# Encoder layer in split f32 on one core: queues of the out-projection and the head, the prompt's last rows, and the end

## The chip, the cores and the metric

The kernel runs on one core of a Trainium2 chip. TensorE (PE) multiplies, with its weight load (PEld) beside it; VectorE (DVE) and ScalarE (ACT) work on tiles in SBUF and PSUM; GpSimd (POOL) and SyncE (SP) here issue transfers only, which 16 DMA engines carry out; ACT issues some too. The metric is device time in microseconds of an execution.

## The reference

One layer of a hybrid encoder, for two sequences that share all weights: a prompt of 512 rows and a sample of 1024 rows, with 2048 columns, in f32.

```python
h = rms_norm(x, norm_g)
z = h @ w_in                         # 2048 x 5632
c_val, c_glu, c_gate, q, k, v, a_gate = split(z)
conv = silu(layer_norm(depthwise_31(c_val * sigmoid(c_glu)))) @ w_pw * silu(c_gate)
attn = banded_sink_attention(rope(q), rope(k), v, sink) * silu(a_gate)
x = x + concat(conv, attn) @ w_out   # 2048 x 2048
y = rms_norm(x, final_norm_g)        # y_prompt, y_sample
```

## The kernel before, in words

**Split products.** A matmul in full f32 is made of three in a rounded f32 type (fp32r): each operand is split in a high part (made by ACT, line 510) and a low part, the operand less its high part (DVE, line 511), and PE adds high x high, high x low and low x high. The method `parts` issues both. Split weights are tiles `hl`, loaded weights `raw`, split tokens (columns of the normalised input) `t`. Where the input is scaled by the norm's gain on the way, ACT does it at line 514 and DVE at line 515.

**Seven products for eight.** For the sample, a `Unit` takes two blocks of weight columns and two of rows and forms the 2x2 block product in seven products P1 to P7 on sums and differences of blocks instead of eight. `make0` to `make3` make the weight operands (differences by `sub`, line 143); `product` (matmuls at line 207) issues one product, 12 matmuls of 128x512; `tap` takes its result out of PSUM. `load0` and `load1` (lines 123 and 127) fetch the raw blocks. The prompt's products are issued by `Job` (line 669), the first unit by `Plain` (line 349).

**Weights that come twice.** The last stage of the prompt needs the same sums and differences of out-projection weights (`w_out`) as the sample made. So where `self.sums` is set, `make1` stores P5, P6 and P4 and `less2` stores P7 to HBM (`wsum_P`, 256 KB each), 64 stores in 16 units. `e.store` (line 504) issues on SP's queue. `load_columns` and the fetch at line 1668 read back later.

**Partial sums.** An out-projection unit is an `Onto`. It works in two passes over the depth: the first half's units write partial outputs (`part_out`), the second half's load them and add onto them (lines 285 and 304), tile names `u` and `g`. `Onto.begin` issues the load; `Onto.ahead` says how many products ahead of the one that needs it (2 for most; for the first two units of the second half it is set by `for u in over[1][:2]`). In the other projections, partial sums go out on POOL (line 268) and are added in memory by an accumulating transfer (line 501).

**The order of the work.** The order of calls gives a sequence of instructions; a scheduler places each on its engine by priority and by when its inputs are expected, and `issue_after` puts an instruction behind another. Loads and stores on SP are one queue, in which an entry that waits holds back those behind it. Hardware DMA completions rotate over eight semaphores, so an issue may also wait for the eighth before it. Functions hung into `before` and `after[step]` of a unit run when the unit has got to that step.

**Prompt's rows.** After the sample's in-projection the prompt's first blocks follow. The prompt's input rows come in 16 pieces, loaded from `xr_d` by `load_two`; `follow(step)` scales and splits pieces 4 step to 4 step + 3 by `prompt.split`, and the last sample unit's (`end`) steps 0 to 3 call it.

**Head.** `first` issues the loads of the first unit on SP: the gain `norm_g` (loaded where the constants are made, line 566), first weight blocks (`plain.load_some`, line 325), and the sample's input (`part`, line 1888); `e.warm` issues filler matmuls (`pt<-ones_r`, line 559) ahead of and between the first real ones.

**End.** `LastPost.last_run` computes the prompt's out-projection, its last group of products at line 1794 for two row blocks t after another, and ends with the final norm of four blocks of 128 rows. `complete` squares a column group with a running sum (line 1735); with the fourth group it takes the square root (ACT, 1745), its reciprocal (1747) and one Newton step (1746, 1748 to 1750), scales the rows by it (1754, 1756, 1758) and stores 512 KB pieces to `y_p` (1759).

## Time and profile before

| | us |
|---|---|
| three runs, median | 2084.76 |
| three runs, lowest to highest | 2084.57 to 2086.94 |
| profiled execution | 2080.18 |
| its span, first to last instruction | 2078.40 |
| PE busy | 2060.7 (99%) |
| DVE, ACT, POOL busy | 1754.4, 1043.6, 122.6 |
| DMA | 494.55 MB, 237 GB/s over the span |

The span is the part of the profiled execution that the trace covers; 1.78 us lie around it. Busy shares are taken over the whole span; a row of the timeline gives start and duration of an instruction or of a run of like instructions, with the idle time ahead of it and what released it. Tile names are printed without numbers.

### The profile page before, as it was taken

The numbers are of one execution on the slowest core, as the hardware profiler recorded it, in microseconds if no ns is written. First come the engines' busy times: TensorE is split into PE (matmuls) and PEld (weight loads), VectorE is DVE, ScalarE is ACT, GpSimd is POOL, SyncE is SP. The second block draws the span as 40 slices with busy tenths as digits, with TensorE's granted clock in tenths as the row PEclk, the third lists the DMA queues.
The fourth block names the chain that finished last, engine by engine and source line by source line (L and its number), as shares of the span: only waits on it lengthen the run. The fifth ranks groups of instructions, "written<-read, shape, count | busy, mean of one in ns | idle before, by whom it ended". The sixth has DMA issues, their size and how long they took to land.

```text
span 2078.4 us, 27092 instructions
## 1 busy us (share of the span) xinstructions
PE 2060.7 (99%) x9259; PEld 1699.2 (82%) x9259; DVE 1754.4 (84%) x2873; ACT 1043.6 (50%) x1711; POOL 122.6 (6%) x176
## 2 busy tenths in 40 slices
PE   9999999999999999999999999999999999999998
PEld 8888888888888888788888888888888887888886
DVE  8767899998899999999666877767799977998887
ACT  7485445333464434554455777336454343454454
POOL 0111111111111111100000000000000000000000
PEclk9999999999999999999999999999999999999999
DMA  8888886864577767954455555996789899678897
GB/s 288 312 298 256 199 223 221 285 220 160 188 242 192 175 169 183 280 166 156 153 172 187 177 182 183 315 330 234 247 289 300 278 299 293 220 247 298 289 333 277
DMA packets 245819, 494.55 MB, mean 238 GB/s; under 512 B 23600, under 2 KB 84400, under 8 KB 245680
## 3 DMA queue, kind: packets, MB, share of 16 engines
q1 hardware_dynamic: 225136, 445.62, 63.9%
q0 software_dynamic: 19392, 45.10, 9.4%
q10 hardware_dynamic: 1152, 2.10, 0.3%
q8 instruction: 72, 1.18, 0.2%
q14 instruction: 67, 0.55, 0.1%
HBM read 331.77 MB, written 160.96 MB: 237 GB/s over the span
## 4 chain that ended last, share of the span: by engine, by line
PE 48%; DVE 7%; issue 6%; DMA 4%; ACT 2%; POOL 1%; SPq 0%; ACTq 0%; POOLq 0%; DVEq 0%
PE a L669 13%; PE a L207 7%; PE c L669 6%; PE b L669 6%; PE c L207 3%; PE pv L1196 2%; PE a L1835 2%; PE s L1167 2%; PE s L1835 2%; PE b L207 1%; PE pt L1201 1%; DVE hl L511 1%; DVE f L1003 1%; DVE t L511 1%; DVE f L1040 1%
## 5 line engine op out<-in xcount | busy, mean ns | idle before, releaser
L207 PE MATMUL a<-t,hl 128*128 128x512 f32 x2640 | 633.6, 391 | 4.7 <-DVE u L304 3.2
L207 PEld LDWEIGHTS a<-t,hl 128*128 128x128 f32 x2640 | 494.7, 188 | 110.6 <-DVE u L304 3.6
L510 ACT ACTIVATE hl<-raw 128x1024 fp32r<-128x1024 f32 (+3 forms) x334 | 296.1, 890 | 384.5 <-PE c L207 81.6
L511 DVE TENSOR_TENSOR hl<-raw,hl 128x1024 fp32r<-128x1024 f32 (+3 forms) x334 | 338.8, 1015 | 145.8 <-ACT hl L510 144.4
L669 PE MATMUL a<-t,hl 128*128 128x512 f32 x1344 | 328.0, 394 | 0.0
L207 PE MATMUL c<-t,hl 128*128 128x512 f32 x1320 | 319.2, 389 | 0.0
L207 PEld LDWEIGHTS c<-t,hl 128*128 128x128 f32 x1320 | 247.3, 188 | 51.6 <-DVE u L304 0.4
L669 PEld LDWEIGHTS a<-t,hl 128*128 128x128 f32 x1344 | 248.6, 188 | 49.8
L1040 DVE SCALAR_TENSOR_TENSOR f<-f,c_w_dw,f 128x512 f32<-128x512 f32 x248 | 173.9, 750 | 0.3
L669 PE MATMUL b<-t,hl 128*128 128x512 f32 x672 | 164.6, 395 | 2.2 <-DVE hl L511 2.2
L1003 DVE SCALAR_TENSOR_TENSOR f<-f,c_w_dw,f 128x512 f32<-128x512 f32 x232 | 163.7, 748 | 1.2 <-ACT f L998 1.2
L669 PE MATMUL c<-t,hl 128*128 128x512 f32 x672 | 164.2, 393 | 0.3 <-DVE hl L511 0.3
L207 PE MATMUL b<-t,hl 128*128 128x512 f32 x660 | 160.0, 389 | 0.0
L669 PEld LDWEIGHTS b<-t,hl 128*128 128x128 f32 x672 | 126.1, 190 | 28.0 <-DVE hl L511 2.6
L669 PEld LDWEIGHTS c<-t,hl 128*128 128x128 f32 x672 | 124.7, 188 | 25.5 <-DVE hl L511 0.7
L207 PEld LDWEIGHTS b<-t,hl 128*128 128x128 f32 x660 | 123.7, 188 | 25.6
L1032 DVE SCALAR_TENSOR_TENSOR f<-f,w_both,f 128x512 f32<-128x512 f32 x120 | 90.0, 750 | 2.1
L236 ACT ACTIVATE u<-a 128x512 f32<-128x512 f32 x82 | 48.7, 594 | 66.8 <-PE a L207 64.2
L236 ACT ACTIVATE g<-a 128x512 f32<-128x512 f32 x78 | 46.3, 594 | 69.1 <-PE a L207 64.6
L1181 ACT ACTIVATE p<-p,tiny 128x384 f32<-128x384 f32 (+1 forms) x96 | 54.5, 570 | 39.8 <-DVE tiny L1178 27.3
L510 ACT ACTIVATE a<-pt 128x512 fp32r<-128x512 f32 x64 | 37.9, 593 | 66.3 <-PE pt L1201 66.2
L511 DVE TENSOR_TENSOR a<-pt,a 128x512 fp32r<-128x512 f32 x64 | 44.1, 689 | 27.3 <-ACT a L510 26.6
(350 smaller groups left out, 2687.9 us busy)
## 6 DMA issues: line engine op xcount, KB each, us to landing
raw<-w_in SPq DMA_DIRECT2D x170, 512.0 KB, 5.3
raw<-w_out SPq DMA_DIRECT2D x31, 512.0 KB, 5.0
raw<-w_pw SPq DMA_DIRECT2D x24, 512.0 KB, 4.2
wsum_P<-raw SPq DMA_DIRECT2D x47, 256.0 KB, 3.3
raw<-wsum_P SPq DMA_DIRECT2D x18, 512.0 KB, 5.0
f<-x_s SPq DMA_DIRECT2D x16, 512.0 KB, 8.2
g<-wsum_P SPq DMA_DIRECT2D x28, 256.0 KB, 4.2
a<-sum_S SPq DMA_DIRECT2D x24, 256.0 KB, 6.2
```

What stands on the lines that cost most here:

```text
L207: nc.tensor.matmul(acc, hl[:, l, o, j, :], toks[j][:, r], start=name in FRESH and j == 0 and q == 0, stop=name in LAST and j == HALF - 1 a ...
L236: nc.scalar.activation(t, bank, AF.Copy)
L510: nc.scalar.activation(hi, x, AF.Copy)
L511: nc.vector.tensor_tensor(lo, x, hi.bitcast(F32), ALU.subtract)
L669: nc.tensor.matmul(job.acc[0], hl[:, l, kk // HALF, kk % HALF, :], r, start=i == 0 and p == 0, stop=i == nk - 1 and p == 2,)
L1003: nc.vector.scalar_tensor_tensor(t, h[:, j : j + T], w(j), t, ALU.mult, ALU.add)
L1032: nc.vector.scalar_tensor_tensor(m0, odd[:, j : j + H], both(j), m0, ALU.mult, ALU.add)
L1040: nc.vector.scalar_tensor_tensor(out, d[:, j : j + H], w(2 * j + k), out if j else m0, ALU.mult, ALU.add)
L1167: nc.tensor.matmul(ps[:, 0:n], qs[:, x, h], k[y][:, keys], start=p == 0, stop=p == 2)
L1181: nc.scalar.activation(p[:, 0:n], p[:, 0:n], AF.Exp, bias=nm[:, h : h + 1], accum_out=l[:, h : h + 1])
L1196: nc.tensor.matmul(pv, v[x][:, vs], pt[:, y], start=i == 0 and p == 0, stop=i == last and p == 2)
L1835: nc.tensor.matmul(acc[t], self.toks[name, m][:, x, i, t * P : (t + 1) * P], parts[i][l].rearrange("p a b -> p (a b)"), start=fresh and fi ...
```

## The change

**Head.** The sample's first half of its first input piece and `norm_g` are loaded from ACT's queue, which removes them from SP's; 13 filler matmuls are asked for instead of 20. **Weight-sum stores.** The 64 stores in `make1` and `less2` are issued by POOL instead of SP. **Out-projection.** The first two units of the second half have `ahead` 1 instead of 0. **Prompt's rows.** The last four pieces (`follow(3)`) are split at step 6 of the last sample unit instead of step 3, behind the last high and low parts made by then. **End.** `complete` no longer scales; it returns a function that does (`scale`). The first block of a pair is scaled at once, the second behind the next block's add and square. The Newton step takes four instead of five DVE operations after the root, since -0.5 is folded into its inputs. The half that holds the last columns goes first, and a block is stored in three pieces, 512 KB and 256 KB on SP and 256 KB on ACT.

```diff
@@ -154,7 +154,7 @@
         self.sub(r1[:, 1], r1[:, 1], t2)
         if self.sums:
             for name, x in (("P5", r1[:, 0]), ("P6", t2), ("P4", r1[:, 1])):
-                self.e.store(self.sums[name], x)
+                self.e.nc.gpsimd.dma_start(self.sums[name], x)
         t = self.e.hl_tile()
         for o, x in enumerate((r1[:, 0], t2)):
             self.e.parts(t[:, 0, o], t[:, 1, o], x)
@@ -163,7 +163,7 @@
     def less2(self):
         self.sub(self.r2[:, 0], self.r2[:, 1], self.r2[:, 0])
         if self.sums:
-            self.e.store(self.sums["P7"], self.r2[:, 0])
+            self.e.nc.gpsimd.dma_start(self.sums["P7"], self.r2[:, 0])
         self.lessened = True

     def make2(self):
@@ -508,6 +508,7 @@
         nc = self.nc
         if g is None:
             nc.scalar.activation(hi, x, AF.Copy)
+            self.high_made = nc.cur_bb.bb.instructions[-1]
             nc.vector.tensor_tensor(lo, x, hi.bitcast(F32), ALU.subtract)
             self.low_made = nc.cur_bb.bb.instructions[-1]
         else:
@@ -566,7 +567,7 @@
             nc.sync.dma_start(t, a[key])
             return t

-        self.norm_g = load("norm_g", [ND])
+        self.norm_g = self.const.tile([P, ND], F32, name="c_norm_g")
         self.ones = self.const.tile([P, P], F32, name="ones")
         nc.vector.memset(self.ones, 1.0)
         self.ones_r = self.const.tile([P, P], F32R, name="ones_r")
@@ -1699,6 +1700,7 @@
         self.gain = {}
         self.sq = [e.small(4) for _ in range(NB)]
         self.rest = [e.small(1) for _ in range(NB)]
+        self.less = [e.small(1) for _ in range(NB)]
         self.load_columns(0, e.A)

     def load_columns(self, c, room):
@@ -1733,6 +1735,7 @@
         self.seen[b] = n + 1
         junk = e.G().rearrange("p (i x) -> p i x", x=P)
         nc.scalar.activation(junk, y, AF.Square, accum_out=self.sq[b][:, n : n + 1])
+        self.squared = nc.cur_bb.bb.instructions[-1]
         if n < 3:
             nc.vector.tensor_tensor(y, y, self.gain[c, odd], ALU.mult)
         sq, rest = self.sq[b], self.rest[b]
@@ -1740,23 +1743,31 @@
             nc.vector.tensor_tensor(rest, sq[:, 0:1], sq[:, 1:2], ALU.add)
             nc.vector.tensor_tensor(rest, rest, sq[:, 2:3], ALU.add)
             nc.vector.tensor_scalar(rest, rest, 1.0 / D, RMS_EPS, ALU.mult, ALU.add)
+            nc.vector.tensor_scalar(self.less[b], rest, -0.5, None, ALU.mult)
         if n == 3:
             s, v, t = e.small(1), e.small(1), e.small(1)
             nc.scalar.activation(s, sq[:, n : n + 1], AF.Sqrt, scale=1.0 / D, bias=rest)
-            nc.vector.tensor_scalar(v, sq[:, n : n + 1], 1.0 / D, rest, ALU.mult, ALU.add)
+            nc.vector.tensor_scalar(v, sq[:, n : n + 1], -0.5 / D, self.less[b], ALU.mult, ALU.add)
             nc.vector.reciprocal(s, s)
             nc.vector.scalar_tensor_tensor(t, s, s, v, ALU.mult, ALU.mult)
-            nc.vector.tensor_scalar(t, t, -0.5, 1.5, ALU.mult, ALU.add)
-            nc.vector.tensor_tensor(s, s, t, ALU.mult)
-            half = self.half
-            for h in range(2):
-                other, last = (self.blocks(self.rows[b], h, o) for o in (1 - odd, odd))
-                nc.scalar.activation(other, other, AF.Identity, scale=s)
-                if h == c:
-                    nc.vector.scalar_tensor_tensor(last, last, s, self.gain[c, odd], ALU.mult, ALU.mult)
-                else:
-                    nc.vector.tensor_scalar(last, last, s, None, ALU.mult)
-                nc.sync.dma_start(self.out[b * P : (b + 1) * P, h * half : (h + 1) * half], self.rows[b][h])
+            nc.vector.scalar_tensor_tensor(s, t, 1.5, s, ALU.add, ALU.mult)
+            return lambda: self.scale(b, c, odd, s)
+
+    def scale(self, b, c, odd, s):
+
+        nc, half = self.e.nc, self.half
+        out = self.out[b * P : (b + 1) * P]
+        other, last = (self.blocks(self.rows[b], c, o) for o in (1 - odd, odd))
+        nc.vector.scalar_tensor_tensor(last, last, s, self.gain[c, odd], ALU.mult, ALU.mult)
+        nc.scalar.activation(other, other, AF.Identity, scale=s)
+        nc.sync.dma_start(out[:, c * half : (c + 1) * half], self.rows[b][c])
+        x = self.rows[b][1 - c]
+        at = (1 - c) * half
+        nc.vector.tensor_scalar(x[:, : half // 2], x[:, : half // 2], s, None, ALU.mult)
+        nc.sync.dma_start(out[:, at : at + half // 2], x[:, : half // 2])
+        nc.scalar.activation(x[:, half // 2 :], x[:, half // 2 :], AF.Identity, scale=s)
+        nc.scalar.dma_start(out[:, at + half // 2 : at + half], x[:, half // 2 :])
+

     ADDS = {
         "P1": ((0, 0),), "P2": ((0, 0),), "P6": ((0, 1),), "P5": ((1, 1),),
@@ -1811,15 +1822,20 @@
                         lane.drain()
                     e.w_prep(len(e.preps))
                     parts = {m: e.hl.pop(at + self.place[c, name, m]) for m in self.PAIRS}
-                    for args in pending:
-                        e.urgently(self.complete, *args)
+                    scales = [e.urgently(self.complete, *args) for args in pending]
                     pending.clear()
+                    e.urgently(scales.pop(0))
                     for t in range(2):
                         for m in self.PAIRS:
                             for i in range(2):
                                 products(t, m, i, parts[m][i])
                         finished(t)
-                        e.urgently(self.complete, *pending.pop())
+                        added = nc.cur_bb.bb.instructions[-1]
+                        scales.append(e.urgently(self.complete, *pending.pop()))
+                        squared = self.squared
+                        while scales:
+                            with e.tc.issue_after(added), e.tc.issue_after(squared):
+                                e.urgently(scales.pop(0))
                     continue
                 before = c == 1 and name == ENDS[c][-2]
                 for n, m in enumerate(self.PAIRS):
@@ -1885,13 +1901,16 @@

     def first():
         x = [e.F([TS]) for _ in range(NF)] + [e.A([TS], F32)]
-        part = lambda k, t: e.nc.sync.dma_start(x[k][:, t * W : t * W + W], sample.xT[k][:, t * W : t * W + W])
+        part = lambda k, t, q=e.nc.sync: q.dma_start(x[k][:, t * W : t * W + W], sample.xT[k][:, t * W : t * W + W])
         plain.begin()
+        part(0, 0, e.nc.scalar)
+        e.nc.scalar.dma_start(e.norm_g, a["norm_g"])
         for k in range(2 * HALF):
             half, j = divmod(k, HALF)
             if j == 0:
                 plain.load_some(0, half, 0, 1)
-            part(k, 0)
+            if k:
+                part(k, 0)
             if j == 0:
                 plain.load_some(1, half, 0, 1)
                 plain.load_some(0, half, 1)
@@ -1901,7 +1920,7 @@
             part(k, 1)
         e.loaded = 2
         e.w_load(3)
-        e.warm(20, True)
+        e.warm(13, True)
         sums = sample.first_sums(x)
         x = None
         for half in range(2):
@@ -2013,8 +2032,13 @@
     end = stages[3][-1]
     end.look = NHL - 1
     end.before.append(last_before)
-    for step in range(4):
+    def follow_last():
+        with e.tc.issue_after(e.high_made), e.tc.issue_after(e.low_made):
+            follow(3)
+
+    for step in range(3):
         end.after[step] = [lambda step=step: follow(step)]
+    end.after[6] = [follow_last]

     pj = prompt.jobs()
     pj[0].behind = pj[0].early = True
@@ -2086,7 +2110,7 @@
         u.next = v
     jobs += grouped(over[0], None) + grouped(over[1], e.A)
     for u in over[1][:2]:
-        u.ahead = 0
+        u.ahead = 1
     over[1][0].next = None
     fj[-1].before.append(lambda: chain[0].begin((0, 0)))
```

On SP, at the turn from the first half of the out-projection to the second. Before, from the last weights of the last first-half unit on (`p<-mix_d` are inputs of the second half, `part_out` its partial sums, written `part_out<-` and read `<-part_out`):

```order
L127 DMA a_14931<-w_out 128x1024
L878 DMA p_14954<-mix_d_198 128x512
L504 DMA wsum_P_0_260<-a_15027 128x4x128
L504 DMA part_out_10_447<-g_14922 128x512
L504 DMA wsum_P_0_264<-raw_14762 128x4x128
L504 DMA wsum_P_0_258<-raw_14822 128x4x128
L878 DMA p_14955<-mix_d_199 128x512
L504 DMA wsum_P_0_262<-a_14931 128x4x128
L878 DMA p_14956<-mix_d_200 128x512
L878 DMA p_14957<-mix_d_201 128x512
L285 DMA u_14962<-part_out_00_417 128x512
L285 DMA g_15019<-part_out_00_421 128x512
```

In the changed kernel, the rows in which the first partial sums are read:

```order
L504 DMA part_out_11_443<-u_14652 128x512
L285 DMA g_14786<-xT_s 128x512
L285 DMA u_14955<-part_out_00_416 128x512
L504 DMA part_out_01_441<-g_14633 128x512
L285 DMA u_15079<-part_out_01_417 128x512
L285 DMA g_14915<-xT_s 128x512
L285 DMA g_15012<-part_out_00_420 128x512
L504 DMA part_out_10_442<-g_14704 128x512
```

and the later rows in which the unit's inputs and last weights stand:

```order
L879 DMA p_14947<-mix_d_198 128x512
L879 DMA p_14948<-mix_d_199 128x512
L504 DMA part_out_01_445<-g_14786 128x512
L879 DMA p_14949<-mix_d_200 128x512
L285 DMA u_15114<-part_out_11_419 128x512
L504 DMA part_out_10_446<-g_14915 128x512
L879 DMA p_14950<-mix_d_201 128x512
L285 DMA u_15224<-part_out_10_418 128x512
L127 DMA a_14924<-w_out 128x1024
L285 DMA g_15095<-part_out_01_421 128x512
```

The first loads of partial sums (`u<-part_out_00`, `g<-part_out_00`) stood behind the last unit's stores and the four inputs; they stand now among the loads of the last first-half unit, ahead of the stores of that before it (`part_out_01` and `_10`). The weight load `a<-w_out` stood ahead of the four `p<-mix_d` and stands now behind them, and the `wsum_P` stores are gone from the queue.

On ACT, where the prompt's first block begins (its high part is the row `hl` from `raw`, 128x1024; the scalings `t` of pieces 12 to 15 read the `a` tiles, those numbered 953 to 955 before and 958 to 961 after). Before:

```order
L514 ACTIVATE t_950_7473<-p_7374,c_norm_g 128x512
L514 ACTIVATE t_953_7495<-a_7406,c_norm_g 128x512
L514 ACTIVATE t_954_7498<-a_7406,c_norm_g 128x512
L514 ACTIVATE t_955_7501<-a_7408,c_norm_g 128x512
L510 ACTIVATE hl_7552<-raw_7347 128x1024
L982 ACTIVATE u_7380<-u_7380 128x512
L982 ACTIVATE g_7414<-g_7414 128x512
L983 DMA gate_d_4_92<-u_7380 128x512
L983 DMA gate_d_6_94<-g_7414 128x512
L418 ACTIVATE hl_7449<-a_7447 128x1024
```

In the changed kernel:

```order
L510 ACTIVATE hl_7533<-raw_7340 128x1024
L983 ACTIVATE g_7407<-g_7407 128x512
L983 ACTIVATE u_7373<-u_7373 128x512
L984 DMA gate_d_6_94<-g_7407 128x512
L984 DMA gate_d_4_92<-u_7373 128x512
L236 ACTIVATE g_7589<-a_7369 128x512
L418 ACTIVATE hl_7576<-raw_7574 128x1024
L515 ACTIVATE t_958_7548<-a_7399,c_norm_g 128x512
L515 ACTIVATE t_959_7551<-a_7399,c_norm_g 128x512
L515 ACTIVATE t_960_7554<-a_7401,c_norm_g 128x512
L515 ACTIVATE t_961_7557<-a_7401,c_norm_g 128x512
L418 ACTIVATE hl_7442<-a_7440 128x1024
```

The scalings of the last rows moved from ahead of the first block's high part to behind two gates (L983) and a further high part. On DVE, in the same place, before:

```order
L257 TENSOR_TENSOR u_7532<-g_7510,u_7532 128x512
L974 TENSOR_TENSOR g_7414<-g_7414,f_1742 128x512
L515 SCALAR_TENSOR_TENSOR t_950_7473<-p_7374,c_norm_g,t_950_7473 128x512
L974 TENSOR_TENSOR u_7380<-u_7380,f_1742 128x512
L257 TENSOR_TENSOR u_7480<-c_7476,u_7480 128x512
L511 TENSOR_TENSOR hl_7552<-raw_7347,hl_7552 128x1024
L1040 SCALAR_TENSOR_TENSOR f_6872<-f_6465,c_w_dw,f_6872 128x512
L515 SCALAR_TENSOR_TENSOR t_953_7495<-a_7406,c_norm_g,t_953_7495 128x512
L515 SCALAR_TENSOR_TENSOR t_954_7498<-a_7406,c_norm_g,t_954_7498 128x512
```

In the changed kernel:

```order
L257 TENSOR_TENSOR u_7513<-g_7491,u_7513 128x512
L975 TENSOR_TENSOR g_7407<-g_7407,f_1735 128x512
L516 SCALAR_TENSOR_TENSOR t_950_7466<-p_7367,c_norm_g,t_950_7466 128x512
L975 TENSOR_TENSOR u_7373<-u_7373,f_1735 128x512
L257 TENSOR_TENSOR u_7473<-c_7469,u_7473 128x512
L512 TENSOR_TENSOR hl_7533<-raw_7340,hl_7533 128x1024
L1041 SCALAR_TENSOR_TENSOR f_6865<-f_6458,c_w_dw,f_6865 128x512 x4
L420 TENSOR_TENSOR hl_7576<-raw_7574,hl_7576 128x512
L516 SCALAR_TENSOR_TENSOR t_958_7548<-a_7399,c_norm_g,t_958_7548 128x512
L516 SCALAR_TENSOR_TENSOR t_959_7551<-a_7399,c_norm_g,t_959_7551 128x512
L516 SCALAR_TENSOR_TENSOR t_960_7554<-a_7401,c_norm_g,t_960_7554 128x512
```

Ahead of the low part (`hl` from `raw`, 128x1024) the five rows are the same; behind it four taps of the depthwise convolution (`f`) and a second low part moved ahead of the last rows.

On SP, the last stores. Before:

```order
L1759 DMA y_p<-a_16701 128x1024
L1759 DMA y_p<-a_16703 128x1024
L1759 DMA y_p<-f_17333 128x1024
L1759 DMA y_p<-f_17335 128x1024
L1759 DMA y_p<-a_16707 128x1024
L1759 DMA y_p<-f_17339 128x1024
L1759 DMA y_p<-a_16709 128x1024
L1759 DMA y_p<-f_17341 128x1024
```

In the changed kernel:

```order
L1763 DMA y_p<-f_17330 128x1024
L1767 DMA y_p<-a_16698 128x512
L1767 DMA y_p<-a_16700 128x512
L1763 DMA y_p<-f_17332 128x1024
L1763 DMA y_p<-f_17336 128x1024
L1767 DMA y_p<-a_16704 128x512
L1763 DMA y_p<-f_17338 128x1024
L1767 DMA y_p<-a_16706 128x512
```

Eight stores of 512 KB (128x1024) became four of these and four of 256 KB, with four more on ACT; the second block's (`a_16700`, `f_17332`) have changed places within the row.

## Prediction, made before the changed kernel was run

> **What bounds the kernel now.** I read the page's head and busy rows first, then the waits of TensorE, then the timelines around each wait. Columns of the page: engine, busy time with its share of the span, instructions; below it a group of instructions with busy time, mean ns of one, and the idle time ahead of it with its releaser.
>
> ```profile
> span 2078.4 us, 27092 instructions
> PE 2060.7 (99%) x9259; PEld 1699.2 (82%) x9259; DVE 1754.4 (84%) x2873; ACT 1043.6 (50%) x1711; POOL 122.6 (6%) x176
> ```
>
> TensorE (PE) is the bound: 2060.7 of 2078.4 us. The change leaves the number of real products alone, so all it can move is the 17.7 us in which PE does nothing, and the stretches in which PE is busy at a lower clock. The waits of PE say who holds it (waiting engine and line, released by, total us, times, longest):
>
> ```profile
> PE a L207 <- DVE u L304: 3.2, 1, 3.2
> PE b L669 <- DVE hl L511: 2.2, 1, 2.2
> PE pt L559 <- DVE ones_r L573: 1.3, 1, 1.3
> PE a L207 <- ACT g L236: 1.1, 1, 1.1
> ```
>
> Each is a single event. 7.8 of the 17.7 us are here; the rest is the start and the end, before PE's first and after its last matmul. A table by windows (length, busy time of PE, PEld, DVE, ACT and POOL with counts, then granted clock, DMA share, GB/s) shows what follows the two long ones:
>
> ```profile
> 1730.00:1736.00 6.00, 6.00 (x21) 4.76 (x20) 5.22 (x9) 2.21 (x3) 0.00 (x0) 0.72 0.81 264
> 1724.00:1730.00 6.00, 2.77 (x12) 1.99 (x11) 3.11 (x5) 2.41 (x4) 0.00 (x0) 1.00 0.92 299
> 860.00:865.00 5.00, 5.00 (x16) 3.92 (x16) 4.01 (x7) 1.81 (x3) 0.88 (x1) 0.66 1.02 264
> ```
>
> After the 3.23 us wait the granted clock is 0.72 over 6.00 us, so 6.00 x 0.28 = 1.68 us are lost again; after the 2.19 us wait it is 0.66 over 5.00 us, 1.70 us. A long wait costs itself plus about 1.7 us.
>
> **Out-projection: units taken up earlier (`ahead` 0 to 1).** The timeline around the 3.23 us wait, rows of SP, DVE and PE (start, us, engine, line, operation, in brackets the idle time before it and its releaser):
>
> ```profile
> 1715.24 0.33 SPq L127 DMA_DIRECT2D a<-w_out  x1
> ...
> 1721.67 1.75 SPq L878 DMA_DIRECT2D p<-mix_d  x2
> 1723.46 0.43 SPq L285 DMA_DIRECT2D u<-part_out  x1
> ...
> 1728.92 0.69 DVE L304 TENSOR_TENSOR u<-a,u 128x512 f32<-128x512 f32 x1 [2.85 <-DMA u<-part_out]
> ...
> 1724.69 1.75 PE L207 MATMUL pt<-t,hl 128*128 128x512 f32 x7
> 1729.67 2.72 PE L207 MATMUL a<-t,hl 128*128 128x512 f32 x8 [3.23 <-DVE u L304]
> ...
> a<-w_out SPq DMA_DIRECT2D x1, 512.0 KB, 3.7
> ```
>
> (The last row is a load's: KB, us to landing.) PE waits for a PSUM bank that DVE empties with an add, and the add waits for `u<-part_out`, a load that SP issued at 1723.46 behind stores of weight sums and of partial outputs. The add began 5.5 us after the issue. With `ahead` at 1 SP issues that load more than one unit earlier (ahead of the last first-half unit's partial stores; a unit is 84 matmuls, some 20 us at the 0.25 of the PE row), so the operand is there long before its add. Gain 3.23 + 1.68 = 4.9 us. PE's order there also returns to taking product P6 before P5, so P6 is due at 1724.69, and it needs the weight difference made from `a<-w_out`. Before, that load left at 1715.24; now it stands behind the four `p<-mix_d`, at 0.88 us each (1.75 for two) 3.5 later, lands 3.7 after that at 1722.4, and three operations of 0.69 (as the add's row) make it ready at 1724.5. SP is rid of six stores of 0.4 on the way, which would make it 1722.0. Between 0.2 and 2.7 us to spare, then: an estimate, and the weakest point of the term. Ends: 4.9 if nothing takes the place, 1.0 if a 2.2 us stall with its clock (3.9) does. I take 4.9, because the late load is the only releaser in the row.
>
> The Trainium skill, "TensorE: Matmul & The Clock Gate", section "Why this matters for your kernels", says that idle gaps of over about 3 us bring TensorE back to half clock. This trace is stricter, since 2.19 us already led to 0.66; by the page a remaining 2.2 us stall would keep the clock and leave 2.7 of this term, by the trace 1.0.
>
> **Weight-sum stores from SP to POOL.** 64 stores of 256 KB, four in each of 16 units. What POOL pays is not shown for this form (128x4x128); nearest rows, and the raw tile's reload (KB, us to landing):
>
> ```profile
> L268 POOL DMA_DIRECT2D part_q<-g x16 | 8.7, 542 | 66.6 <-DVE g L257 60.3 <-ACT g L236 6.2
> L501 POOL DMA_DIRECT2D u<-part_q x16 | 15.0, 940 | 63.0 <-DVE u L257 55.2 <-issue 7.8
> ...
> raw<-w_out SPq DMA_DIRECT2D x31, 512.0 KB, 5.0
> ```
>
> A plain 256 KB store takes POOL 0.54 us, an accumulating one 0.94. The moved store writes pieces a quarter as long, so its ends are 0.54 and 4 x 0.54 = 2.2 us; I take 0.9, near the dearer row. POOL is 6% busy and has nothing of the out-projection queued behind it, so 64 x 0.9 = 58 us of POOL lie beside PE. The price is in the buffers: the raw tile of a stored sum is loaded anew only when the store has landed. One unit's case:
>
> ```profile
> 1687.16 0.37 SPq L504 DMA_DIRECT2D wsum_P<-raw  x1
> ...
> 1699.46 0.33 SPq L127 DMA_DIRECT2D raw<-w_out  x1
> ...
> 1707.52 0.69 DVE L143 TENSOR_TENSOR raw<-raw,raw 128x512 f32<-128x512 f32 x1
> ```
>
> The stores begin at 1687.16; the reload goes out at 1699.46 and lands 5.0 us later, 3.1 us before DVE uses it at 1707.52. Four stores one after the other may therefore take 1699.5 - 1687.2 + 3.1 - 5 = 10.4 us, 2.6 each, before they delay a product. Cost at 0.9 or at 2.2: nothing, hidden by products of PE. If POOL takes longer, that cover is gone, in all 16 units. SP in turn loses 64 rows of about 0.4 us and the semaphore waits around them; SP is nowhere the bound but at the load above, so I count no gain beyond that one.
>
> **Prompt's last rows behind the first block.** The 2.19 us wait, rows of DVE, ACT and PE, and the load (KB, us to landing):
>
> ```profile
> 854.05 0.70 DVE L257 TENSOR_TENSOR u<-g,u 128x512 f32<-128x512 f32 x1
> 855.74 0.69 DVE L974 TENSOR_TENSOR g<-g,f 128x512 f32<-128x512 f32 x1 [1.00 <-DMA g<-part_gate]
> ...
> 858.21 1.22 DVE L511 TENSOR_TENSOR hl<-raw,hl 128x1024 fp32r<-128x1024 f32 x1
> ...
> 855.46 1.04 ACT L510 ACTIVATE hl<-raw 128x1024 fp32r<-128x1024 f32 x1
> ...
> 859.49 2.91 PE L669 MATMUL b<-t,hl 128*128 128x512 f32 x8 [2.19 <-DVE hl L511]
> ...
> g<-part_gate POOLq DMA_DIRECT2D x1, 256.0 KB, 9.0
> ```
>
> The change takes three of ACT's scalings from in front of the high part (855.46), which so begins some 2 us sooner (0.72 each, by the scaling's row under the head); the low part on DVE still has the same five operations ahead of it, led by the one that waited until 855.74 for `g<-part_gate`, 9.0 us under way. PE waits for the low part at 858.21 + 1.22. No load is moved ahead of that transfer, and POOL's accumulation itself stays where it is, so the low part comes at the same time: gain 0; ends 0 and 2.7 (the 1.00 us of that idle time, and the clock's 1.70 if the shorter wait spares it). The moved scalings (four on ACT, four on DVE; their two loads stay where they were) go behind the first block, beside its products; the second block's high part now stands behind them on ACT, some 3 us later (4 x 0.72), and the first block's products, which still start after the same wait, cover that.
>
> **Head.** SP's first issues, the first matmuls, and ACT's first scaling:
>
> ```profile
> 0.74 0.39 SPq L566 DMA_DIRECT2D c_norm_g<-norm_g  x1
> 1.19 0.42 SPq L325 DMA_DIRECT2D raw<-w_in  x1
> 1.66 0.42 SPq L1888 DMA_DIRECT2D f<-xT_s  x1
> ...
> 4.67 0.72 ACT L514 ACTIVATE t<-f,c_norm_g 128x512 fp32r<-128x512 f32 x1 [1.15 <-DMA f<-xT_s]
> ...
> 6.61 1.05 PE L349 MATMUL a<-t,hl 128*128 128x512 f32 x2
> ...
> 10.65 0.84 PE L349 MATMUL b<-t,hl 128*128 128x512 f32 x3
> ```
>
> Two issues leave SP for the idle ACT queue: two slots of 0.46 us, so SP's later loads go out 0.9 us sooner, and the first scaling, which waited for `f<-xT_s` until 4.67, follows them. PE's matmuls up to 10.65 take about twice those after it (1.05 for two against 0.84 for three), and real work is interleaved with filler `pt` matmuls, of which seven go. Work gained at half rate is worth half, and the weights' transfers share the same DMA engines, so of 0.9 us I take 0.6; ends 1.0 and, if the seven missing fillers let the full clock begin later, -1.7 as after the waits above.
>
> **End.**
>
> ```profile
> 2069.48 0.74 DVE L1756 SCALAR_TENSOR_TENSOR f<-f,tiny,u 128x512 f32<-128x512 f32 x1
> 2070.15 0.68 DVE L1726 TENSOR_TENSOR f<-a,f 128x512 f32<-128x512 f32 x1
> 2071.62 0.21 DVE L1746 TENSOR_SCALAR tiny<-tiny,tiny 128x1 f32<-128x1 f32 x1 [0.79 <-ACT g L1735]
> ...
> 2072.78 0.49 DVE L1758 TENSOR_SCALAR a<-a,tiny 128x512 f32<-128x512 f32 x1
> ...
> 2073.53 0.33 SPq L1759 DMA_DIRECT2D y_p<-a  x1
> 2074.14 0.33 SPq L1759 DMA_DIRECT2D y_p<-f  x1
> ```
>
> The last block's add at 2070.15 stood behind the scaling of the block before; with that done earlier it starts 0.3 us sooner, at the last matmul's end. The Newton step loses one operation of 0.2 us out of the chain from 2071.62 to 2072.78. The first store so leaves about 0.5 us sooner. From then on 1 MB at DMA rate runs to 2078.4, and three pieces carry the same bytes; the second block's stores, now later, may still be in the way. I take 0.4; ends 1.0 (the last piece 0.6 sooner as well) and -0.6 (a third issue in line, 0.33, and a queue not yet empty).
>
> **Sum.** 0.6 + 4.9 + 0 + 0 + 0.4 = 5.9 us. The profiled execution took 2080.18 us (its span and 1.78 around it), which becomes 2074.3; the median of the three runs, 2084.76, lies 4.58 above the profiled one, and the same 5.9 make it 2078.9.
>
> **The rivals.** *The first block's wait shrinks too.* It needs `g<-part_gate` to land 1.0 us sooner, for which only the reshuffled order of the loads around it speaks, and against which its own unmoved place on POOL does. 2.7 more, 2076.2.
>
> *The out-projection's wait only moves* to the weights behind `p<-mix_d`, or a wait of 2.2 us appears where the order of ACT and DVE has changed (beside the attention, 860 to 1050, and before the tail). For it: as little as 0.2 us of slack. Against: PE waited four times in 2000 us. 3.9 us less gain: 2082.8; twice, 2086.7.
>
> *Slower: the stores hold the raw tiles.* Place: each of 16 units; it decides at 2.6 us for a store. Each 0.1 us over it delays the last of four by 0.4, 6.4 us over 16 units, so at 2.8 us (12.8 us) the time is 2091.7. Against it: 0.54 and 0.94 in the rows, taken while DVE was 84% busy. The Trainium skill, "SBUF — State Buffer", section "SBUF: two separate sides", warns that a DMA issued from POOL can stand still while DVE holds the port they share; no POOL row here is stretched that way (0.54 and 0.94).
>
> *The change does nothing in the large*: the head's and the end's 1.0 us alone, 2083.8, if the late load finds another queue to wait in; it goes with the second rival.
>
> **How the numbers follow.** Two medians of this kernel can be told apart from about 0.2%, 4.2 us: faster means under 2080.6, slower over 2088.9. Forecast as summed 0.57 (one time in ten of it short of 4.2), first rival 0.08, a moved or new wait 0.25 (mostly within the 4.2), stores 0.10. Faster: 0.51 + 0.08 = 0.59, and 0.01 of single waits that cost less than 2.2. Slower: stores and three or more new waits, 0.14. Same: the remaining 0.26. The range goes from the first rival with the upper ends of head and end (2076.2 - 1.0 = 2075.2) to two new waits, 2086.7; the likeliest case alone spans 2077 to 2081.
>
> **What would show it.** In the changed profile PE's wait for `u` at L304 must be gone, the clock after the place stay at 1.0, and `u<-part_out` be issued about 25 us ahead of its add; the wait at `hl` L511 must remain near 2.2 us, with DVE's add behind `g<-part_gate`; POOL's new stores must take 0.5 to 2.2 us with no wait of DVE on `raw`; the first real matmul must start before 5.65, and the last store leave before 2074.14 less what was gained ahead. The prediction is wrong if PE waits for weight parts at the turn of the out-projection, if a new wait of 2 us stands anywhere, or if a POOL store takes over 2.6 us.

## The result, and the profile after

| | us |
|---|---|
| kernel before, median of four runs | 2084.83 (2084.57 to 2086.94) |
| changed kernel, median of four runs | 2118.9 (2115.88 to 2122.32) |
| ratio, 95% interval | 1.0163 [1.0146, 1.018] |
| span of the profiled execution, before and after | 2078.4 and 2119.4 |

The change costs 34 us. The head of the page of the changed kernel, with the stores' group as POOL issues them (busy us, mean ns):

```profile
span 2119.4 us, 27184 instructions
PE 2073.3 (98%) x9252; PEld 1703.7 (80%) x9252; DVE 1751.5 (83%) x2873; ACT 1042.4 (49%) x1711; POOL 170.2 (8%) x240
...
L157 POOL DMA_DIRECT2D wsum_P<-raw x32 | 24.3, 758 | 856.2 <-DVE raw L143 765.0
```

DVE, ACT and PE do the same work. The two profiled spans lie 41.0 us apart, more than the medians: PE's idle time grows from 17.7 to 46.1 us, and its busy time, at a lower clock, by 12.6. The waits of PE after:

```profile
PE a L207 <- DVE u L304: 11.4, 3, 9.0
PE c L207 <- DVE u L304: 6.8, 2, 3.7
PE b L670 <- DVE hl L512: 2.8, 1, 2.8
PE pv L1197 <- DVE a L512: 2.7, 2, 2.4
PE a L1851 <- DVE f L1594: 2.3, 1, 2.3
PE a L207 <- ACT hl L510: 2.0, 1, 2.0
```

The stretch from 1500 to 1900 us, most of the sample's out-projection, as a row of the windows before and then after (length, busy PE, PEld, DVE, ACT, POOL, then granted clock, DMA share, GB/s):

```profile
1500.00:1900.00 400.00, 396.55 (x1783) 327.93 (x1782) 360.57 (x582) 183.88 (x312) 0.00 (x0) 1.00 0.84 277
```

```profile
1500.00:1900.00 400.00, 374.56 (x1644) 304.43 (x1643) 330.08 (x545) 167.32 (x287) 48.55 (x64) 0.97 0.75 251
```

Here PE is busy 396.55 - 374.56 = 22.0 us less. Its 1644 matmuls take 0.2278 us each, against 0.2224 before; that is 8.9 us in the lower clock behind the waits. Together 31 of the 41 us between the two profiled spans lie in this stretch, where the 64 stores are.

What POOL does with them shows in its timeline. The bracket is the idle time ahead of each store:

```profile
1677.60 0.76 POOL L157 DMA_DIRECT2D wsum_P<-raw  x1 [5.14 <-DVE f L1004]
1683.29 0.76 POOL L157 DMA_DIRECT2D wsum_P<-raw  x1 [4.93 <-DVE a L512]
1689.67 0.76 POOL L157 DMA_DIRECT2D wsum_P<-g  x1 [5.63 <-issue]
1695.99 0.76 POOL L166 DMA_DIRECT2D wsum_P<-raw  x1 [5.55 <-DVE u L304]
1699.66 0.76 POOL L157 DMA_DIRECT2D wsum_P<-raw  x1 [2.92 <-issue]
1705.99 0.76 POOL L157 DMA_DIRECT2D wsum_P<-raw  x1 [5.58 <-DVE g L143]
```

A store is busy for 0.76 us, and the next follows only 3.7 to 6.4 us after it began; the releasers named are whatever ended near that moment, and two are "issue", nothing that the profile shows. The landings tell more: the store of 1683.29 lands at 1689.37, and the next begins at 1689.67. Of the 63 stores behind the first, 50 begin 0.30 to 0.36 us after the landing of the store ahead of them, and none begins sooner.

SP pays for it. Its waits for such a store to land at the reload of raw tiles (L127), before and then after:

```profile
SPq L127 <- DMA wsum_P<-raw: 8.5, 5, 2.9
```

```profile
SPq L127 <- DMA wsum_P<-raw: 62.4, 13, 8.5
```

At L127 thirteen reloads stand 62.4 us for a store to land, where five stood 8.5 us before. Seven loads of `g` tiles (L285) add 31.8 us and five of raw tiles (L123) 18.7, where one of each stood 1.4 and 0.7 before; SP's queue stands with them. The longest stall, on POOL, SP, ACT, DVE and PE:

```profile
1719.73 0.76 POOL L166 DMA_DIRECT2D wsum_P<-raw  x1 [6.72 <-issue]
...
1723.45 0.33 SPq L123 DMA_DIRECT2D raw<-w_out  x1
1723.88 2.17 SPq L879 DMA_DIRECT2D p<-msum_S  x4
...
1729.66 0.33 SPq L127 DMA_DIRECT2D raw<-w_out  x1
...
1728.88 0.63 ACT L510 ACTIVATE t<-p 128x512 fp32r<-128x512 f32 x1 [11.52 <-DMA p<-msum_S]
...
1732.51 1.23 DVE L512 TENSOR_TENSOR hl<-raw,hl 128x1024 fp32r<-128x1024 f32 x1 [9.46 <-ACT hl L510]
...
1735.09 2.47 PE L207 MATMUL a<-t,hl 128*128 128x512 f32 x5 [8.97 <-DVE u L304]
```

The store of 1719.73 lands at 1723.39, and the raw tile's load leaves at 1723.45. The inputs `p<-msum_S` stand on SP behind that load; ACT's high parts wait for them, and behind ACT wait DVE and PE.

### The profile page after: what moved, and what is told of

It is laid out like the page before. It is cut to its first block, busy times and chain, and to the rows that moved or that the text cites. A ratio compares the mean times of both kernels' runs of the same rounds, so it can differ in the third digit from the quotient of the medians.

```text
span 2119.4 us, 27184 instructions
## 1 busy us (share of the span) xinstructions
PE 2073.3 (98%) x9252; PEld 1703.7 (80%) x9252; DVE 1751.5 (83%) x2873; ACT 1042.4 (49%) x1711; POOL 170.2 (8%) x240
## 3 DMA queue, kind: packets, MB, share of 16 engines
q0 software_dynamic: 24512, 61.88, 11.6%
## 4 chain that ended last, share of the span: by engine, by line
PE 38%; DVE 12%; issue 9%; DMA 7%; ACT 1%; POOL 1%; SPq 0%; DVEq 0%; POOLq 0%; ACTq 0%
PE a L670 12%; PE b L670 6%; PE c L670 5%; DVE hl L512 2%; PE s L1851 2%; PE pv L1197 2%; PE a L1851 2%; PE s L1168 2%; PE a L207 2%; PE pt L1202 1%; DMA a<-ag_d 1%; DVE f L1004 1%; DVE t L512 1%; PE c L207 1%; DVE raw L143 1%
## 5 line engine op out<-in xcount | busy, mean ns | idle before, releaser
L157 POOL DMA_DIRECT2D wsum_P<-raw x32 | 24.3, 758 | 856.2 <-DVE raw L143 765.0
```

## The experiments

Ratios are to the kernel before, on the same chip, with 95% intervals; its medians there were 2085.5 to 2086.6, its single runs 2077.38 to 2096.85, so a difference of medians under 2 us says little. The ratio is the recorded one, not the quotient of two medians (for the head that would be 1.0015).

| kernel | median us | ratio |
|---|---|---|
| changed kernel, stores back on SP | 2087.43 | 1.0006 [0.9993, 1.0018] |
| kernel before, only the stores on POOL | 2119.08 | 1.0165 [1.0147, 1.0184] |
| changed kernel, ring of 1152 bytes | 2083.42 | 0.9991 [0.998, 1.0002] |
| changed kernel, stores in 2 KB pieces | 2083.75 | 0.9992 [0.9983, 1.0002] |
| changed kernel, stores on ACT's queue | 2084.23 | 0.9994 [0.9984, 1.0004] |
| kernel before, ahead 1 alone | 2086.41 | 1.0007 [0.9991, 1.0023] |
| kernel before, head alone | 2089.76 | 1.0008 [0.9995, 1.0022] |
| kernel before, prompt's rows alone | 2086.65 | 1.0002 [0.999, 1.0014] |
| kernel before, end alone | 2085.15 | 0.9993 [0.9982, 1.0004] |

### Which part costs it

Stores back on SP, all else changed:

```diff
-                self.e.nc.gpsimd.dma_start(self.sums[name], x)
+                self.e.store(self.sums[name], x)
-            self.e.nc.gpsimd.dma_start(self.sums["P7"], self.r2[:, 0])
+            self.e.store(self.sums["P7"], self.r2[:, 0])
```

> The changed kernel with its 64 weight-sum stores back on SP; the other parts stay. Theory 1 (the stores on POOL hold the raw tiles: POOL's rows in the changed kernel show 0.76 us a store, but the next one follows only 3.0 to 6.7 us later): the loss is gone, 2079 to 2085 us, and PE's waits in the out-projection fall from 28 us to under 3. Theory 2 (the reordered loads of ahead 1, or the prompt's rows, starve PE): still 2105 or more.

Measured: 1.0006. And the reverse, the same two lines turned in the kernel before and nothing else:

> The kernel before with only the 64 stores moved to POOL. Theory 1: slower by about as much as the whole change, 2112 to 2125 us, with POOL's stores 3 to 6.7 us apart. Theory 2: 2080 to 2090.

Measured: 1.0165, the whole change's 1.0163. The stores on POOL are the loss, and the other four parts together are nothing that can be measured. Theory 2 falls.

### What holds the stores

The kernel's source sets `dynamic_dma_scratch_size`, read here as the space for the descriptions of POOL's transfers (the ring). The first trial makes it an eighth larger:

```diff
-... dynamic_dma_scratch_size=1024)
+... dynamic_dma_scratch_size=1152)
```

> The changed kernel with 1152 instead of 1024 bytes per partition reserved for POOL's transfer descriptors (72 of 16 bytes in place of 64). Each store is 512 pieces, 32 for each of 16 DMA engines, and one more that signals. Theory 1a (the next store waits for room in that ring, which holds one store and not two): 66 fit into 72, so two stores are under way at once, successive stores of a unit can follow within 1 to 3 us, and the time falls well below 2118.9, to 2085 to 2105. Theory 1b (POOL itself needs 3 to 6 us to write 512 descriptors, or DVE keeps it from writing): no change, 2115 to 2122.

Measured: 0.9991; 128 bytes give back the loss. POOL in that kernel, one unit's four stores:

```profile
1669.16 0.75 POOL L157 DMA_DIRECT2D wsum_P<-raw  x1 [13.18 <-DVE raw L143]
1670.96 0.76 POOL L157 DMA_DIRECT2D wsum_P<-g  x1 [1.05 <-DVE g L143]
1673.69 0.75 POOL L166 DMA_DIRECT2D wsum_P<-raw  x1 [1.97 <-DVE a L512]
1674.97 0.76 POOL L157 DMA_DIRECT2D wsum_P<-raw  x1 [0.53 <-DVE hl L512]
```

The unit's four stores need 6.6 us from the first start to the end of the last, where the same unit's four in the changed kernel took 15.4 (1662.98 to 1678.36). The second follows its operand; the third begins 0.31 us after the first has landed (1673.38), the fourth 0.30 after the second (1674.67). In this kernel 48 of 63 stores begin ahead of the landing of the store before them; 30 begin 0.30 to 0.34 us after the landing of the store two before, and none sooner than that. SP's waits at L127 for stores fall from 62.4 to 21.4 us. The pieces, DVE's work and POOL's code are the same in both, so theory 1b (POOL's own writing, or DVE's hold) falls: 0.75 us is what the writing costs, and what followed it was a wait for the transfer ahead, one store at a time with 1024 bytes and two with 1152. The Trainium skill, "DMA: Bandwidth & Descriptors", sections "Terms" and "SWDGE vs HWDGE vs iDMA", says that a descriptor has 16 bytes and that POOL's are written to rings in SBUF. By that figure 1024 bytes are 64 and 1152 are 72, an estimate. SP's queue counted 528 packets for such a store, 33 for each of 16 engines; if a store from POOL takes 33 descriptors too, two are 66. That one store fits into 64 and two into 72 agrees with both traces; the page gives no size limit, and how many descriptors a store from POOL takes was not read directly.

The second trial leaves the space and takes fewer pieces, by a layout in which a partition's 2 KB lie together:

```diff
-... dram(f"wsum_{p}", [2 * HALF, W], 2) ...
+... dram(f"wsum_{p}", [2, W // P, HALF, P], 2) ...
-... d[c][:, HALF * g : HALF * g + HALF, n * P : n * P + P] ...
+... d[c][:, g, n] ...
```

> The changed kernel with the stored sums laid out in HBM so that a partition's 2 KB lie together (128 pieces a store, 8 for each DMA engine, in place of 512); the prompt's last stage then reads them in pieces of 512 bytes, 18 of its loads as two. Stores stay on POOL. Theories 1a and 1b, if the number of pieces is what costs: POOL's stores can follow one another after 1 to 2 us, the waits of the out-projection are gone, 2078 to 2086. If DVE's hold on POOL costs, whatever the pieces: 2105 or more.

Measured: 0.9992. POOL's group in it, and two stores in a row:

```profile
L157 POOL DMA_DIRECT2D wsum_P<-raw x32 | 17.4, 542 | 914.4 <-DMA f<-msum_S 671.4 <-DVE raw L143 200.2 <-DVE tiny L1187 40.4
...
1693.59 0.54 POOL L166 DMA_DIRECT2D wsum_P<-raw  x1
1694.19 0.54 POOL L157 DMA_DIRECT2D wsum_P<-raw  x1
```

0.60 us from one to the next, with no idle time; 27 stores here begin before the store two ahead of them has landed, which none does with 1152 bytes and 512 pieces. With the stores off SP and no ring in the way, the first partial sums are loaded early here, and PE's wait in this stretch is another; DVE and PE:

```profile
1711.99 1.22 DVE L512 TENSOR_TENSOR hl<-raw,hl 128x1024 fp32r<-128x1024 f32 x1 [3.53 <-ACT hl L510]
...
1714.57 7.36 PE L207 MATMUL a<-t,hl 128*128 128x512 f32 x24 [1.81 <-DVE u L304]
```

The add `u` stands on DVE behind a weight's low part, that behind ACT's high part. The third trial asks whether 512-byte pieces are slow beside loads whoever issues them:

```diff
-                self.e.nc.gpsimd.dma_start(self.sums[name], x)
+                self.e.nc.scalar.dma_start(self.sums[name], x)
```

(and the same for P7)

> The changed kernel with its 64 stores on ACT's queue instead of POOL's, pieces of 512 bytes as before. Theory 1a (the ring of POOL's transfers is what holds them; ACT's queue has none): no stores 3 to 6.7 us apart, so the loss is gone, 2079 to 2088, less well than on POOL's queue with wide pieces, since ACT waits for DVE's differences before each store. Rival (512-byte stores beside loads, whoever issues them): 2100 or more.

Measured: 0.9994. The rival falls: ACT's queue takes the same pieces without loss. It did as well as POOL with wide pieces, not less well.

### The other parts, one at a time

```diff
-        u.ahead = 0
+        u.ahead = 1
```

> The kernel before with ahead 1 for the first two units of the out-projection's second half, nothing else. If the prediction's term is right (ahead 1 brings the load of the first partial sums forward): PE's 3.2 us wait at L304 is gone, 4.9 us less than the kernel before. Rival: the load was brought forward by taking the stores off SP, not by ahead, as the order of SP in this kernel has it where it was: the wait stays near 3 us and the time is the same within 1 us.

Measured: 1.0007. SP, DVE and PE in it:

```profile
1726.33 0.44 SPq L285 DMA_DIRECT2D u<-part_out  x1
...
1731.88 0.69 DVE L304 TENSOR_TENSOR u<-a,u 128x512 f32<-128x512 f32 x1 [3.06 <-DMA u<-part_out]
...
1732.62 5.49 PE L207 MATMUL a<-t,hl 128*128 128x512 f32 x12 [4.18 <-DVE u L304]
```

The load leaves 5.6 us ahead of its add, as before (5.5), and PE waits 4.18 us. In SP's queue it stands behind the four `p<-mix_d`, in this kernel as in the one before, and also in the changed kernel with its stores on SP. It moves forward in each kernel whose stores left SP, also in the one with only the stores on POOL, where `ahead` is 0. The rival holds.

The head alone (the first two pieces of the diff that concern `norm_g`, `part` and `warm`):

```diff
-        self.norm_g = load("norm_g", [ND])
+        self.norm_g = self.const.tile([P, ND], F32, name="c_norm_g")
+        part(0, 0, e.nc.scalar)
+        e.nc.scalar.dma_start(e.norm_g, a["norm_g"])
-        e.warm(20, True)
+        e.warm(13, True)
```

> The kernel before with the head's part alone (two loads on ACT's queue, 13 fillers). The prediction's term: 0.6 us less, with PE's first real matmul before 5.65. Rival: with seven fillers fewer PE stands still before the first real matmul (1.06 us in the changed kernel, at 5.41) and the full clock begins later: 0 to 1.7 us more. Neither can be told by the time; the start of the tenth and later matmuls and the clock in the first 20 us tell it.

Measured: 1.0008. PE in it:

```profile
5.33 0.80 PE L349 MATMUL a<-t,hl 128*128 128x512 f32 x1 [0.97 <-ACT t L514]
...
13.39 0.84 PE L349 MATMUL b<-t,hl 128*128 128x512 f32 x3
```

The first real matmul starts at 5.33 in place of 5.65, after 0.97 us of standing still, and the group that began at 13.38 before begins at 13.39. The full speed comes at about 11.3 here and 10.65 before, so the gain is spent within 8 us; that the missing fillers cause the later change of speed was not shown, since with the same fillers it came at 9.4 in the kernel with the larger ring. One pair of executions does not settle the head's worth: over the fourteen profiled ones that group begins at 12.71 to 13.41 us in the six without the head's part and at 12.15 to 13.57 in the eight with it.

The prompt's last rows alone:

```diff
-    for step in range(4):
+    for step in range(3):
         end.after[step] = [lambda step=step: follow(step)]
+    end.after[6] = [follow_last]
```

> The kernel before with the prompt's last rows behind its first block, nothing else. The prediction's term: 0, with PE's wait at hl L511 still 2.2 us and DVE's add behind the load of g from part_gate. Rival (the changed kernel waited 2.85 there): the reordering makes it longer, 0.7 us more.

Measured: 1.0002, and the wait is there, with the same load ahead of it (DVE waits for it at 860.49):

```profile
860.49 0.69 DVE L975 TENSOR_TENSOR g<-g,f 128x512 f32<-128x512 f32 x1 [1.93 <-DMA g<-part_gate]
...
862.97 1.22 DVE L512 TENSOR_TENSOR hl<-raw,hl 128x1024 fp32r<-128x1024 f32 x1
...
864.24 4.10 PE L670 MATMUL b<-t,hl 128*128 128x512 f32 x11 [3.12 <-DVE hl L512]
```

The end alone (the diff's `complete`, `scale` and `last_run`):

> The kernel before with the end's part alone. The prediction's term: 0.4 us less from PE's last matmul to the end of the span (8.6 us before), last store issued 0.5 us sooner. Rival (stores of the second block, now later, keep the DMA engines full): no gain or up to 0.6 us more.

Measured: 0.9993, no difference that can be told. From PE's last matmul (2073.95) to the end of the span (2083.0) it takes 9.05 us, against 8.62 before, though the first of the last stores leaves 3.31 us after that matmul, against 3.75. The share of DMA from the last matmul on, in 40 slices, before and then in this kernel:

```profile
DMA  9999999999999999900008999999999992000000
```

```profile
DMA  9989899999899999999999999999999200000000
```

Before, the engines had drained (zeros) when the last block's 1 MB came; with the end's part they are full all the way. That this makes the end longer does not follow: in the seven profiled executions with the end as it was, the engines drain in each, and the time from PE's last matmul on is 8.6 to 10.5 us; in the six with the changed end it is 8.6 to 9.2. The 8.62 is the shortest of the first kind. Whether ACT's queue adds to it was asked with the third piece on SP:

```diff
-        nc.scalar.dma_start(out[:, at + half // 2 : at + half], x[:, half // 2 :])
+        nc.sync.dma_start(out[:, at + half // 2 : at + half], x[:, half // 2 :])
```

> The kernel before with the end's part, its third store of a block on SP's queue in place of ACT's. The end's part took 9.05 us from PE's last matmul to the end of the span against 8.62 before, though the first of the last stores left 0.44 us sooner. Theory A (the second queue's last store ends later): back to 8.2 to 8.7. Theory B (the second block's stores, moved behind the third's square, keep the DMA engines full up to the last store): still 9.0 or more.

In its one execution PE's last matmul ends at 2076.54 and the span at 2085.8: 9.26 us. That speaks against theory A. It does not show theory B, since 9 us and more is also what the end as it was takes in six of its seven profiled executions.

### Two versions from what was learned

DVE's multiply behind the late load, put behind the first block's low part:

```diff
     end.look = NHL - 1
+    end.landing = 6
```

> The stores on POOL in 2 KB pieces, the head's part, ahead 1 and the prompt's last rows behind its first block; the end as before. New: the last sample unit hands its finished sums on two products later (landing 6 in place of 4), so on DVE the multiply that waits for the load of g from part_gate stands behind the first prompt block's low part. Theory (that multiply, 1.0 us of waiting and 0.6 of its own, holds the low part): the wait at hl L512 falls from 2.2 to 3.3 us to 0.6 to 1.7, and the kernel is 4 to 8 us under the one before, 2078 to 2082 on the scale of its 2086. Rival (ACT's high part or the loads set it): the wait stays above 2 us, and the time stays where the wide stores had it, 2.3 us below.

Measured: 1.0012 [1.0, 1.0023]. PE and ACT at the place:

```profile
862.00 5.29 PE L670 MATMUL b<-t,hl 128*128 128x512 f32 x22 [0.47 <-DVE hl L512]
869.82 5.74 PE L670 MATMUL b<-t,hl 128*128 128x512 f32 x24 [2.54 <-ACT hl L418]
...
865.92 1.06 ACT L418 ACTIVATE hl<-raw 128x1024 fp32r<-128x1024 f32 x1 [3.95 <-DMA raw<-w_in]
```

The first wait fell to 0.47 us, as the theory has it, and one block later PE waits 2.54 us for weights that SP loads: the stall moved on, and nothing is won. The stores in wide pieces with the end as before, which is this kernel without `landing`:

> The changed kernel with stores on POOL in 2 KB pieces and the end as it was before (the end's part took 9.05 us behind the last matmul, 8.62 before). Theory: 0.4 us below the wide stores, which were 2.3 us under the kernel before; ratio 0.997 to 1.000. Rival: runs of one kernel differ by more than the parts, and nothing under 0.2% is seen.

Measured: 2085.17, 1.0006 [0.9997, 1.0016]; its rival holds. In its trace the load of `g` was in time, PE's first wait is 1.09 us without `landing`, and no wait of 2.5 us follows; from the last matmul to the end it takes 10.2 us. So the comparison for the 0.47 us is this 1.09 as well as the 2.2 before. No version tried is faster than the kernel before by what can be told: the best four end 0.06 to 0.09% below it, with intervals that reach over 1.

## Why the prediction was wrong

It forecast 2078.9 within 2075.2 to 2086.7; the time is 2118.9.

- **Stores on POOL: wrong, and this is the loss.** The step that failed is the price of a store, 0.9 us between the ends 0.54 and 2.2, taken from POOL's busy rows. The busy row was right (0.76), and not the price: POOL began the next store 3.7 to 6.4 us after it in the rows shown. The third rival named the place (the raw tiles) and the point (2.6 us for a store), which the pitch passes, but gave it 0.10 for the sake of those rows. Its mechanism was another, too: neither DVE nor the shared port holds POOL, as the larger ring shows with DVE's work unchanged. The rows used were of stores with 128 pieces, several of which fit at once; the form with 512 pieces had no row, and its upper end should have been the time for which a transfer lasts, as if they went one by one. The page of the kernel before has that time, from issue to landing on SP, and it is over the 2.6 us:

```profile
wsum_P<-raw SPq DMA_DIRECT2D x47, 256.0 KB, 3.3
```

- **The rival's size: too large.** 6.4 us for each 0.1 us over 2.6 would be over 100 us at a pitch of 5; it was 34. The formula made all 16 units pay four times the excess; at L127 13 reloads waited, 4.8 us each at the mean (62.4 us), and most of SP's waiting lay beside PE's products, since PE lost 22 us of busy time in the stretch.
- **Out-projection, 4.9 us: wrong step.** The step "with `ahead` at 1 SP issues that load more than one unit earlier" gave to one part what another did: the order shown was of all parts together. By itself ahead 1 leaves the load where it was. With the stores off SP and no ring to wait for, the load is early, and PE then waits 1.64 (larger ring) or 1.81 us (wide pieces) some 15 us sooner, at an add that stands behind a weight's parts. In three more kernels with the stores off SP that wait is 2.6 us (landing 6), 1.4 (stores on ACT) or absent (wide pieces with the end as before). So the wait was gone in one of these five traces and moved and shorter in four, and the second rival, the wait that only moves, was right in part.
- **Prompt's rows, 0: right**, by its own reason: DVE waits for `g<-part_gate` (1.93 us in the kernel with this part alone, 1.71 in the changed one) and the low part keeps its place behind it. PE's wait is DVE's and about 1.2 us more: 1.00 and 2.19 before, 1.93 and 3.12 with this part alone, 1.71 and 2.85 in the changed kernel. With DVE's multiply moved away (landing 6) the next block's weights were late, by 2.54 us.
- **Head, 0.6: not shown.** The first matmul came 0.32 us earlier, and in that pair nothing of it was left at 13.4 us. Over all traces the same group begins within 0.7 us without the head's part and within 1.4 with it, so neither the time nor the traces can tell 0.6.
- **End, 0.4: open.** The store left 0.44 us earlier as worked out; in that pair the end came 0.43 later, within the given ends (-0.6 to 1.0). Over all traces the end as it was takes 9.5 us at the mean and the changed one 9.0, with a spread of 1.9 us in the first; so neither a gain of 0.4 nor a loss is shown.
- **The clock** was priced at 1.7 us behind each long wait, and 8.9 us are lost in it in the stretch. The price does not hold for each wait: behind the changed kernel's waits of 2.45 us (from 1605.40 on) and 2.07 us (from 1663.90 on) the granted clock is 1.00 over 6.00 us, behind those of 3.09 and 1.97 us (1633.93 and 1805.32) it is 0.72, and behind that of 8.97 us it is 0.52. Which waits of 2 us lower the clock is open.

## What to carry to other kernels

The busy row of a POOL transfer was here the time to write it down, not the time until the next one could be written: look at the pitch of back-to-back transfers of the same form, and where none is in the trace, take the transfer's whole duration as the upper end. Before many small-piece stores go to POOL, make their pieces longer, or its reserved space larger, or use ACT's queue: each of the three took the loss away here. An order that is changed by five parts at once says nothing of which part moved a row; build the parts alone before one of them is given the gain.

## What the runs showed of the hardware

128 bytes more of reserved space for POOL's transfers, of 1024, decided 35 us: with 1024 a 512-piece store kept the next one waiting until 0.30 us after its own landing, with 1152 two went at once and the third waited for the first's (why, by descriptors, is the estimate above). A store from POOL also counts 80 packets whether it is 512 pieces or 128 (24512 on its queue in both kernels, against 19392 without the 64 stores), while SP counted about 528 for each (225136 against 191344 with only the stores moved to POOL).
